# Second FFN matrix of a two-layer streaming encoder by seven block products, with an adding transfer for one weight sum

## Chip, cores and metric

The kernel runs on one core of one Trainium2 chip. The metric is the device time of one execution in microseconds (us), from the first to the last instruction of the core and the little around it; of several runs the median is given.

## What is computed

One step of an encoder of two layers on 544 tokens (512 of a prompt, 32 of a later chunk) with 1024 features. Cut to what matters here:

```python
def swiglu(x, w_in, w_out):                  # w_in 1024 x 5632, w_out 2816 x 1024
    gate, up = jnp.split(x @ w_in, 2, axis=-1)
    return (jax.nn.silu(gate) * up) @ w_out

def encoder_layer(x, ...):
    x = layer_norm(ALPHA * x + 0.5 * swiglu(x, w_ffn_in[0], w_ffn_out[0]), ln_g[0], ln_b[0])
    ...                                      # mix = mixers(x @ w_in) @ w_out
    x = layer_norm(ALPHA * x + mix, ln_g[1], ln_b[1])
    x = layer_norm(ALPHA * x + 0.5 * swiglu(x, w_ffn_in[1], w_ffn_out[1]), ln_g[2], ln_b[2])
```

So there are four FFNs, two in each layer, with a mixer between the two. All is float32.

## The kernel before

Features lie on the 128 partitions, tokens on the free dimension: x is 8 tiles of 128 features x 544 tokens, and a matmul covers one half of the tokens, 272 columns (`HS`). For float32 accuracy each operand is split into a rounded high part (ACT, `S.activation` with Copy, L174 for weights, L286 for data) and the rest (DVE, L175, L287), and each product is three matmuls: high x high, low x high, high x low (L254, L258, L342).

An FFN has 22 inner features of 128 (`NF`). `plan` (L573) sets the order: `FSPLIT = (8, 7, 7)` cuts the inner features into three parts; a part's features are made, then, one feature later, the part's share of the second matrix (w2) is added to y for all 8 outputs. Below, a *w1 unit* is one inner feature, a *w2 stage* one part's pass over the outputs.

- **First matrix.** Features 0 and 1 (`NPLAIN`) are plain products. Features 2 to 21 are made by seven products of blocks in place of eight (`seven` L333, `hidden` L547): the blocks are the two halves of the 8 inputs, the two token halves, and gate and up. `Blocks.add` (L313) makes the sums of x's blocks once for an FFN (four DVE operations of 272 columns and two splits per pair of tiles), `Weights.sums` (L209) the sums of the weights' blocks for each unit (four DVE operations of 512 columns, `add` L204, and seven splits). 84 matmuls make a unit.
- **Second matrix.** Plain: for each output m, n features x 2 halves x 3 matmuls, then two additions to y on DVE (`resid` L450).
- **Last part and layer norm** (`out_phase` L458). The third w2 stage carries the layer norm with it. After output 1 a rough mean of output 0 is taken by a matmul (`shift`, L371) and subtracted; from there on each finished output is shifted (DVE L378), squared (ACT L380), and added into two sums by POOL (`add`, L381 and L382). POOL also prepares the held back outputs (`before`, L389). The last two outputs (four in the kernel's last norm) are held back as `tail`: half 0 of all of them first, added on DVE (`add_last` L394 to L397), then the statistics of half 0 by matmuls (`stats` L403, L408), the centring and scaling (`centre` L427, `spread` L419 and L422, `scale` L433, L438), and the new x (ACT L443, POOL L444). `start` (L525) begins the next matrix's first two products, tile by tile, as the new x comes.
- **Weights.** `Weights` (L158) loads on the SP queue, in the order of use, into 3 raw tiles of 1024 columns (`RAW_BUFS`), and splits into 10 pairs of tiles of 512 columns (`W_BUFS`). `get` keeps one or two units ahead of the use (`ahead`, L235).

Each engine executes in order; the program's scheduler sets that order from the code and the tiles that come free.

Of the kernel before, what the change touches and what calls it, by code (L numbers as in the profile page):

```python
# [10 lines left out]
F32 = mybir.dt.float32  # L11
# [59 lines left out]
def encoder_kernel(  # L71
# [6 lines left out]
    w2: bass.AP,  # L78
    wi: bass.AP,
# [19 lines left out]
    xp = ctx.enter_context(tc.tile_pool(name="xp", bufs=34))  # L99
# [48 lines left out]
    class Tile:  # L148


        def __init__(self, groups):
            self.groups = groups

        def at(self, k):
            g, c = k // 4, k % 4
            return tuple(v[:, c * P:(c + 1) * P] for v in self.groups[g])

    class Weights:  # L158

# [6 lines left out]
        def fetch(self):  # L166
            return wp.tile([P, NK * P], F32, tag="raw", name="raw", bufs=RAW_BUFS)

        def group(self, raw):

            n = raw.shape[-1]
            hi = wp.tile([P, G], F32R, tag="whi", name="whi", bufs=W_BUFS)
            lo = wp.tile([P, G], F32R, tag="wlo", name="wlo", bufs=W_BUFS)
            S.activation(out=hi[:, :n], in_=raw, func=AF.Copy)  # L174
            V.tensor_tensor(out=lo[:, :n], in0=raw, in1=hi[:, :n].bitcast(F32), op=ALU.subtract)  # L175
            return hi, lo

        def blocks(self, src):
            out = []
            for i in range(2):  # L180
                raw = self.fetch()
                nc.sync.dma_start(out=raw, in_=src[:, 2 * i * G:2 * (i + 1) * G])
                out += [raw[:, :G], raw[:, G:]]
            return out

        def load(self):
            kind, src, n = self.units[self.loaded]
            self.loaded += 1
            if kind == "t":
                raw = self.fetch()  # L190
                nc.sync.dma_start(out=raw[:, :n], in_=src)
                out = Tile([self.group(raw[:, g:min(g + G, n)]) for g in range(0, n, G)])
            elif kind == "p":
                out = self.pair([self.group(b) for b in self.blocks(src)])
            else:
                out = self.sums(src)
            self.ready.append(out)

        @staticmethod
        def pair(groups):  # L200
            b11, b12, b22, b21 = groups
            return [Tile([b11, b21]), Tile([b12, b22])]

        def add(self, a, b):  # L204
            r = big["pool"].tile([P, G], F32, tag="sum", name="sum", bufs=4)
            V.tensor_tensor(out=r, in0=a, in1=b, op=ALU.add)  # L206
            return r

        def sums(self, src):  # L209
            b11, b12, b22, b21 = self.blocks(src)  # L210
            g11, g21 = self.group(b11), self.group(b21)
            r1 = self.add(b11, b12)
            r2 = self.add(r1, b22)
            g2, g1 = self.group(r2), self.group(r1)
            g3 = self.group(self.add(b12, b22))
            g22 = self.group(b22)
            return g11, g21, g2, g1, g3, g22, self.group(self.add(r2, b21))

        def first(self, x):

            src, n = self.units[0][1], G
            out = []
            for i in range(NK // 4):
                ks = slice(4 * i, 4 * i + 4)
                nc.sync.dma_start(out=ya[:, ks, HS[0]], in_=xT[:, ks, HS[0]])
                raw = self.fetch()
                for c in range(2):
                    nc.sync.dma_start(out=raw[:, c * n:(c + 1) * n], in_=src[:, (2 * i + c) * n:(2 * i + c + 1) * n])
                for k in range(NK)[ks]:
                    split(y[k], x[k], HS[0])  # L230
# [908 lines left out]
```

## Time and profile before

| | us |
|---|---|
| median of 3 runs | 2022.68 |
| lowest, highest | 2021.6, 2023.53 |
| the profiled execution | 2021.5 |
| its span, first to last instruction | 2019.7 |
| mean granted TensorE clock, share of full speed | 0.985 |
| stages of the first FFN, by PE: w1 features 2 to 8 | 44.13 to 118.51 |
| first w2 stage (8 features) | 118.51 to 166.51 |
| w1 features 9 to 15 | 166.51 to 240.06 |
| second w2 stage (7 features) | 239.90 to 281.98 |
| w1 features 16 to 21 | 281.98 to 345.02 |
| third w2 stage with the norm, up to the mixer's first matmul | 344.86 to 391.23 |

The profile is one execution. Its views: a page of totals; windows, which give each engine's busy time in a stretch; groups of instructions by line; a timeline; the waits; the chain of work that ended last, followed backwards. A duration on PE or DVE overlaps its neighbours, so the cost of one more instruction is read from the distance between starts.

### The profile page before, as it was taken

Reading aid. Unit: us, or ns where it says so; the run is one execution under the profiler, and the core shown is the slowest. Engines: PE = TensorE matmul, PEld = TensorE weight load, DVE = VectorE, ACT = ScalarE, POOL = GpSimd, SP = SyncE. Lnnn points to the kernel's source line nnn. Section 1 sums busy time; section 2 is a strip of 40 time slices with the busy share of each in tenths; the row PEclk is TensorE's granted clock in tenths of the full one; section 3 lists DMA queues with packets and bytes.
Section 4 is the critical chain, followed back from the end, with each engine's and each line's share of the span. In section 5 each row is a group of like instructions: output and inputs, shape, how many; then the busy total and the mean of one; then the engine's idle time right before and its main releaser. Section 6 shows DMA issues by size and latency. Waiting matters only on the chain.

```text
span 2019.7 us, 37955 instructions
## 1 busy us (share of the span) xinstructions
PE 1974.7 (98%) x15326; PEld 1935.6 (96%) x15326; DVE 1476.5 (73%) x2854; ACT 1002.9 (50%) x2009; POOL 225.1 (11%) x216
## 2 busy tenths in 40 slices
PE   7999999999998999999999999999999989999997
PEld 7999999999998999999999999999999989999997
DVE  7957767777658966858698586777766599577677
ACT  5634535465435543526366254455644366345353
POOL 0000000510224000000320000015001320000003
PEclk9999999999999999999999999999999999999999
DMA  6332323142221332323313323232421213323231
GB/s 199 105 105 85 105 85 110 58 152 92 64 84 32 115 105 84 100 87 101 100 52 107 94 95 109 81 104 85 136 96 55 84 39 108 105 84 105 88 102 45
DMA packets 61752, 189.09 MB, mean 94 GB/s; under 512 B 8932, under 2 KB 13156, under 8 KB 61576
## 3 DMA queue, kind: packets, MB, share of 16 engines
q1 hardware_dynamic: 52592, 173.18, 27.0%
q10 hardware_dynamic: 8984, 13.49, 2.1%
q8 instruction: 120, 1.97, 0.4%
q14 instruction: 56, 0.46, 0.1%
HBM read 179.88 MB, written 8.34 MB: 93 GB/s over the span
## 4 chain that ended last, share of the span: by engine, by line
PE 89%; DVE 6%; ACT 2%; DMA 1%; issue 1%; POOL 1%; SPq 0%; ACTq 0%
PE b L342 41%; PE b L254 28%; PE b L258 14%; DMA raw<-in_w 1%; PE b L773 1%; PE b L772 1%; DVE wlo L175 1%; PE o L788 1%; DVE z L433 1%; POOL xl L444 1%; ACT ya L438 1%; ACT whi L174 1%; DVE sum L206 1%; DVE ya L427 1%; PE b L753 0%
## 5 line engine op out<-in xcount | busy, mean ns | idle before, releaser
L174 ACT ACTIVATE whi<-raw 128x512 fp32r<-128x512 f32 x576 | 353.8, 618 | 510.8 <-PE b L258 304.6
L175 DVE TENSOR_TENSOR wlo<-raw,whi 128x512 fp32r<-128x512 f32 x576 | 403.2, 703 | 165.6 <-ACT whi L174 161.7
L254 PE MATMUL b<-hh,whi 128*128 128x272 f32 x1408 | 405.7, 288 | 0.0
L254 PE MATMUL b<-hh,wlo 128*128 128x272 f32 x1408 | 405.5, 288 | 0.0
L258 PE MATMUL b<-hl,whi 128*128 128x272 f32 x1408 | 404.7, 287 | 0.0
L174 ACT ACTIVATE whi<-sum 128x512 fp32r<-128x512 f32 x320 | 200.9, 631 | 210.8 <-PE b L258 100.0
L254 PE MATMUL b<-xh,whi 128*128 128x272 f32 x896 | 270.4, 306 | 24.8 <-ACT sg L591 12.2
L175 DVE TENSOR_TENSOR wlo<-sum,whi 128x512 fp32r<-128x512 f32 x320 | 218.7, 688 | 87.4 <-ACT whi L174 79.9
L342 PE MATMUL b<-xh,wlo 128*128 128x272 f32 x960 | 276.2, 288 | 0.0
L342 PE MATMUL b<-xh,whi 128*128 128x272 f32 x960 | 276.1, 288 | 0.0
L342 PE MATMUL b<-xl,whi 128*128 128x272 f32 x960 | 275.2, 287 | 0.0
L254 PEld LDWEIGHTS b<-hh,whi 128*128 128x128 f32 x1408 | 265.0, 188 | 0.1
L254 PEld LDWEIGHTS b<-hh,wlo 128*128 128x128 f32 x1408 | 264.9, 188 | 0.1
L258 PEld LDWEIGHTS b<-hl,whi 128*128 128x128 f32 x1408 | 264.8, 188 | 0.0
L254 PE MATMUL b<-xh,wlo 128*128 128x272 f32 x896 | 261.7, 296 | 0.3 <-DVE wlo L175 0.3
L258 PE MATMUL b<-xl,whi 128*128 128x272 f32 x896 | 248.1, 297 | 1.4 <-POOL xl L444 1.4
L254 PEld LDWEIGHTS b<-xh,whi 128*128 128x128 f32 x896 | 175.1, 196 | 30.5 <-ACT xh L443 13.5
L342 PE MATMUL b<-s56h,whi 128*128 128x272 f32 x640 | 184.5, 288 | 1.3 <-ACT up L552 1.3
L342 PE MATMUL b<-s73h,whi 128*128 128x272 f32 x640 | 184.6, 288 | 0.6 <-ACT sg L552 0.6
L342 PE MATMUL b<-s56h,wlo 128*128 128x272 f32 x640 | 184.5, 289 | 0.0
L342 PE MATMUL b<-s73h,wlo 128*128 128x272 f32 x640 | 183.9, 287 | 0.0
L342 PE MATMUL b<-s73l,whi 128*128 128x272 f32 x640 | 183.9, 287 | 0.0
(220 smaller groups left out, 4177.7 us busy)
## 6 DMA issues: line engine op xcount, KB each, us to landing
raw<-in_w SPq DMA_DIRECT2D x206, 512.0 KB, 3.7
raw<-in_w SPq DMA_DIRECT2D x64, 448.0 KB, 3.3
raw<-in_wi SPq DMA_DIRECT2D x40, 512.0 KB, 3.3
raw<-in_wo SPq DMA_DIRECT2D x16, 512.0 KB, 3.3
U<-scr ACTq DMA_DIRECT2D x8, 320.0 KB, 3.4
out_nkT<-k ACTq DMA_DIRECT2D x8, 272.0 KB, 2.4
out_nvT<-vT ACTq DMA_DIRECT2D x8, 272.0 KB, 2.1
out_yT<-ya SPq DMA_DIRECT2D x16, 136.0 KB, 1.8
```

What stands on the lines that cost most here:

```text
L174: S.activation(out=hi[:, :n], in_=raw, func=AF.Copy)
L175: V.tensor_tensor(out=lo[:, :n], in0=raw, in1=hi[:, :n].bitcast(F32), op=ALU.subtract)
L206: V.tensor_tensor(out=r, in0=a, in1=b, op=ALU.add)
L254: PE.matmul(acc[:, :HALF], v, x[k][0][:, HS[h]], start=first and i == 0, stop=False)
L258: PE.matmul(acc[:, :HALF], w.at(k)[0], x[k][1][:, HS[h]], start=False, stop=last)
L342: PE.matmul(acc[:, :HALF], v[:, cs], x, start=opens and j == 0 and m == 0, stop=j == len(xs) - 1 and m == 2, skip_group_check=True)
L427: eng.tensor_tensor(out=c, in0=c, in1=self.mean[h], op=ALU.subtract)
L433: V.tensor_tensor(out=z, in0=c, in1=self.rstd[h], op=ALU.mult)
L438: S.activation(out=c, in_=z, func=AF.Identity, bias=b, scale=g)
L444: POOL.tensor_tensor(out=xl[:, sl], in0=c, in1=xh[:, sl].bitcast(F32), op=ALU.subtract)
L772: PE.matmul(g[:, :w], qc[c][parts[c], qs], kh[parts[c], :w], start=True, stop=False)
L773: PE.matmul(g[:, :w], qc[c][:, qs], kc[c][:, :w], start=False, stop=True)
```

## The change

The second matrix is also computed by seven products for 18 of the 22 inner features. `FSPLIT = (6, 6, 6, 4)`: three parts of 6 features by seven products, the last 4 features plainly, in `out_phase`. The blocks are pairs of outputs (m, m+1), pairs of inner features (even, odd), and token halves. `Blocks.add` now also makes the sums of a pair of inner features (L327 to L330 of the changed kernel), and `resid7` adds the seven products to y. A unit of w2 has three column groups per block, so 384 columns. In `sums` one of the four additions, r3 = b12 + b22, is made by a DMA transfer that POOL issues and that adds onto the loaded tile; the others are laid out on double tiles of 1024 columns, the splits still on at most 512 columns each. Features 0 and 1 come as plain tiles, the sums of x's blocks are made after feature 0 is evacuated, and buffers are cut anew: 4 raw tiles, 4 double pairs, 26 instead of 34 tiles of data plus 16 of one half.

```diff
-FSPLIT = (8, 7, 7)
+FSPLIT = (6, 6, 6, 4)
-W_BUFS = 10
-RAW_BUFS = 3
+W_BUFS = 4
+RAW_BUFS = 4
...
-        def sums(self, src):
-            b11, b12, b22, b21 = self.blocks(src)
-            g11, g21 = self.group(b11), self.group(b21)
-            r1 = self.add(b11, b12)
-            r2 = self.add(r1, b22)
-            g2, g1 = self.group(r2), self.group(r1)
-            g3 = self.group(self.add(b12, b22))
-            g22 = self.group(b22)
-            return g11, g21, g2, g1, g3, g22, self.group(self.add(r2, b21))
+        def part(self, raw, hi, lo):
+            n = raw.shape[-1]
+            for c in (slice(0, n // 2), slice(n // 2, n)) if n > G else (slice(0, n),):
+                S.activation(out=hi[:, c], in_=raw[:, c], func=AF.Copy)
+                V.tensor_tensor(out=lo[:, c], in0=raw[:, c], in1=hi[:, c].bitcast(F32), op=ALU.subtract)
...
+        def sums(self, src, n):
+
+            a, b = self.fetch()[:, :2 * n], self.fetch()[:, :2 * n]
+            u, v = slice(0, n), slice(n, 2 * n)
+            nc.sync.dma_start(out=b, in_=src[:, 2 * n:])
+            nc.sync.dma_start(out=a, in_=src[:, :2 * n])
+            POOL.dma_start(out=b[:, u], in_=src[:, 3 * n:], accum_op=ALU.add)
+            ga = self.group(a)
+            r = big["pool"].tile([P, 2 * G], F32, tag="sum", name="sum", bufs=2)[:, :2 * n]
+            V.tensor_tensor(out=r[:, u], in0=a[:, u], in1=b[:, u], op=ALU.add)
+            V.tensor_tensor(out=r[:, v], in0=r[:, u], in1=b[:, v], op=ALU.subtract)
+            gr, gb = self.group(r), self.group(b)
+            V.tensor_tensor(out=a[:, v], in0=r[:, u], in1=a[:, v], op=ALU.add)
+            g4 = tuple(wp.tile([P, G], F32R, tag=f"{t}4", name=f"{t}4", bufs=1)[:, :n] for t in ("hi", "lo"))
+            self.part(a[:, v], *g4)
+            return [tuple(t[:, c] for t in g) for g in (ga, gr, gb) for c in (u, v)] + [g4]
...
+    def resid7(m, alpha):
+
+        seen = set()
+
+        def step(i, h, op):
+            def f(acc):
+                c = y[m + i][:, HS[h]]
+                if alpha and (i, h) not in seen:
+                    V.scalar_tensor_tensor(out=c, in0=c, scalar=ALPHA, in1=acc, op0=ALU.mult, op1=op)
+                else:
+                    V.tensor_tensor(out=c, in0=c, in1=acc, op=op)
+                seen.add((i, h))
+            return f
...
     def ffn(l, f, x, pre):
-        xb = Blocks(x)
-        hs = []
+        xb = Blocks(x[:NK // 2], x[NK // 2:])
...
-                hs.append(new_x("h"))
-                split(sg, hs[-1])
+                n = i - starts[last]
+                if n >= 0:
+                    tail.append(new_x("h") if n else new_b("h"))
+                    split(sg, tail[-1])
+                elif i % 2 == 0:
+                    if i in starts:
+                        parts.append(Blocks([], []))
+                    hb = parts[-1]
+                    hb.first.append(new_h("h", 1))
+                    split_half(sg, hb.first[-1], 0)
+                    held = sg
+                else:
+                    hb.second.append(new_x("h"))
+                    split(sg, hb.second[-1])
+                    hb.add(held, sg, new_x)
+                if i == 0:
+                    for k in range(NK // 2):
+                        xb.add(y[k], y[k + NK // 2], new_b)
                 continue
...
-            for m in range(NK):
-                acc = run(mm2(W.get(), part, range(n)))
-                for h in range(2):
-                    resid(m, acc[h], h, i == 0)
+            if i == last:
+                return out_phase(l, 2 * f, tail, range(FSPLIT[i]), False)
+            for m in range(0, NK, 2):
+                seven(W.get(), parts[i], resid7(m, i == 0))
```

What the instructions' order becomes is shown at two places. The first is DVE in the first w2 stage. Names: ya is y, wlo the low part of a weight, sum and raw the sums and loaded blocks of weights, b a PSUM bank. Before:

```order
L454 SCALAR_TENSOR_TENSOR ya<-ya,b 128x272
L175 TENSOR_TENSOR wlo<-raw,whi 128x512
L454 SCALAR_TENSOR_TENSOR ya<-ya,b 128x272
L206 TENSOR_TENSOR sum<-sum,raw 128x512
L175 TENSOR_TENSOR wlo<-raw,whi 128x512
L206 TENSOR_TENSOR sum<-raw 128x512
L454 SCALAR_TENSOR_TENSOR ya<-ya,b 128x272
L175 TENSOR_TENSOR wlo<-raw,whi 128x512
L206 TENSOR_TENSOR sum<-sum,raw 128x512
L454 SCALAR_TENSOR_TENSOR ya<-ya,b 128x272
```

Now, from the middle of one pair of outputs to the middle of the next:

```order
L208 TENSOR_TENSOR raw<-sum,raw 128x384
L600 SCALAR_TENSOR_TENSOR ya<-ya,b 128x272
L602 TENSOR_TENSOR ya<-ya,b 128x272
L177 TENSOR_TENSOR wlo<-sum,whi 128x384 x2
L600 SCALAR_TENSOR_TENSOR ya<-ya,b 128x272
L205 TENSOR_TENSOR sum<-raw 128x384
L600 SCALAR_TENSOR_TENSOR ya<-ya,b 128x272
L177 TENSOR_TENSOR wlo<-raw,whi 128x384 x2
L602 TENSOR_TENSOR ya<-ya,b 128x272
L206 TENSOR_TENSOR sum<-sum,raw 128x384
L602 TENSOR_TENSOR ya<-ya,b 128x272
L177 TENSOR_TENSOR wlo<-raw,whi 128x384 x2
```

Two additions to y and a split or sum alternated before, and the sums belonged to the next w1 unit; now ten operations on weights of 384 columns and seven additions stand in each pair of outputs, and the sum of raw blocks (L205), which needs the adding transfer, stands between additions of the pair before it.

The second place is POOL at the passage from the mixer to the second FFN. Before (L413 is a power for the norm, L444 the low part of the new x, L389 the next norm):

```order
L413 TENSOR_TENSOR rstd<-var,mhalf 68x4
L444 TENSOR_TENSOR xl<-ya,xh 128x272 x5
L413 TENSOR_TENSOR rstd<-var,mhalf 68x4
L444 TENSOR_TENSOR xl<-ya,xh 128x272 x11
L389 TENSOR_TENSOR ya<-ya,shift 128x544 x2
```

Now (L423, L454 the same; L202 is the adding transfer):

```order
L423 TENSOR_TENSOR rstd<-var,mhalf 68x4
L454 TENSOR_TENSOR xl<-ya,xh 128x272 x4
L423 TENSOR_TENSOR rstd<-var,mhalf 68x4
L454 TENSOR_TENSOR xl<-ya,xh 128x272 x11
L202 DMA raw<-in_w 128x512
L454 TENSOR_TENSOR xl<-ya,xh 128x272
L202 DMA raw<-in_w 128x512 x3
L202 DMA raw<-in_w 128x384 x4
```

An adding transfer has moved ahead of the last of sixteen low parts, and the others follow in the stages in which POOL had no instruction.

## Rows read from the trace of the kernel before

**Rows 1.** The page, part 1: each engine's busy time, share and instructions.
```profile
PE 1974.7 (98%) x15326; PEld 1935.6 (96%) x15326; DVE 1476.5 (73%) x2854; ACT 1002.9 (50%) x2009; POOL 225.1 (11%) x216
```

**Rows 2.** The page, part 4: the chain that ended last, by engine and by line.
```profile
PE 89%; DVE 6%; ACT 2%; DMA 1%; issue 1%; POOL 1%; SPq 0%; ACTq 0%
PE b L342 41%; PE b L254 28%; PE b L258 14%; DMA raw<-in_w 1%; PE b L773 1%; PE b L772 1%; DVE wlo L175 1%; PE o L788 1%; DVE z L433 1%; POOL xl L444 1%; ACT ya L438 1%; ACT whi L174 1%; DVE sum L206 1%; DVE ya L427 1%; PE b L753 0%
```

**Rows 3.** Windows by stage: from:to and length, each engine's busy us (instructions), clock, DMA.
```profile
118.51:166.51 48.00, 48.00 (x387) 48.00 (x386) 23.24 (x42) 10.78 (x17) 0.00 (x0) 1.00 0.27 87
166.51:240.06 73.55, 73.55 (x591) 73.55 (x590) 61.92 (x110) 44.34 (x83) 0.00 (x0) 1.00 0.32 98
...
344.86:391.23 46.37, 44.27 (x360) 43.83 (x358) 32.48 (x60) 18.79 (x35) 20.01 (x13) 1.00 0.27 87
```

**Rows 4.** Timeline of PE: start, us, line, operation, tiles, count [idle before].
```profile
355.34 0.41 PE L371 MATMUL o<-rough,ones 128*128 128x272 f32 x2
...
383.27 0.62 PE L403 MATMUL o<-acc,onesd 128*128 128x272 f32 x2
...
391.23 0.40 PE L254 MATMUL b<-xh,whi 128*128 128x272 f32 x1 [2.11 <-ACT xh L443]
```

**Rows 5.** Timeline of POOL in the same stage.
```profile
356.71 3.72 POOL L389 TENSOR_TENSOR ya<-ya,shift 128x544 f32<-128x544 f32 x2 [356.27 <-DVE wlo L175]
...
373.41 1.69 POOL L381 TENSOR_TENSOR acc<-acc,ya 128x544 f32<-128x544 f32 x1 [1.80 <-DVE ya L378]
...
379.92 1.38 POOL L382 TENSOR_TENSOR acc<-acc,sq 128x544 f32<-128x544 f32 x1
```

**Rows 6.** Groups by line of POOL: count | busy us, mean ns | idle.
```profile
L382 POOL TENSOR_TENSOR acc<-acc,sq 128x544 f32<-128x544 f32 x28 | 41.3, 1475 | 0.0
L381 POOL TENSOR_TENSOR acc<-acc,ya 128x544 f32<-128x544 f32 x22 | 35.5, 1615 | 37.5 <-DVE ya L378 37.5
```

**Rows 7.** Timelines of POOL, DVE, PE in the last FFN's end.
```profile
1971.98 5.03 POOL L389 TENSOR_TENSOR ya<-ya,shift 128x544 f32<-128x544 f32 x3 [327.31 <-DVE wlo L175]
...
1986.65 1.35 POOL L382 TENSOR_TENSOR acc<-acc,sq 128x544 f32<-128x544 f32 x1
...
1986.72 1.59 DVE L396 TENSOR_TENSOR acc<-acc,ya 128x272 f32<-128x272 f32 x1 [1.98 <-POOL acc L381]
...
1993.40 0.62 PE L403 MATMUL o<-acc,onesd 128*128 128x272 f32 x2
```

**Rows 8.** Window of DVE where the second FFN begins: busy us (instructions), PEclk, DMA.
```profile
640.00:693.60 53.60, 53.06 (x101) 1.00 0.25 79
```

**Rows 9.** Window of PE behind the hole at 391.23: busy us (instructions), PEclk, DMA.
```profile
391.23:398.10 6.87, 6.87 (x38) 0.54 0.00 0
```

**Rows 10.** Waits of PE: us in total, times, longest us.
```profile
PE b L254 <- ACT sg L591: 12.2, 3, 8.1
```

**Rows 11.** DMA issues: count, KB each, median us to landing.
```profile
raw<-in_w SPq DMA_DIRECT2D x206, 512.0 KB, 3.7
...
ck<-in_ckT ACTq DMA_DIRECT2D x8, 256.0 KB, 4.3
...
Us<-scr ACTq DMA_DIRECT2D x8, 68.0 KB, 2.9
par_sb<-in_par SPq DMA_DIRECT2D x1, 474.0 KB, 10.0
```

**Rows 12.** Timeline of DVE in a w2 stage.
```profile
257.31 0.43 DVE L456 TENSOR_TENSOR ya<-ya,b 128x272 f32<-128x272 f32 x1
257.65 0.55 DVE L175 TENSOR_TENSOR wlo<-raw,whi 128x384 fp32r<-128x384 f32 x1
258.12 0.69 DVE L206 TENSOR_TENSOR sum<-raw 128x512 f32<-128x512 f32 x1
258.72 0.69 DVE L206 TENSOR_TENSOR sum<-sum,raw 128x512 f32<-128x512 f32 x1
```

**Rows 13.** Groups by line of DVE.
```profile
L175 DVE TENSOR_TENSOR wlo<-raw,whi 128x384 fp32r<-128x384 f32 x64 | 38.9, 608 | 12.2 <-ACT whi L174 10.7
```

More of the change, by code (lines that the diff above doesn't have):

```diff
@@ L189, in load @@
             if kind == "t":
[L190 to L194, printed above, removed]
-            else:
[L196 to L202, printed above, removed]
@@ L229, in first @@
                 for k in range(NK)[ks]:
-                    split(y[k], x[k], HS[0])
-                out += [self.group(raw[:, c * n:(c + 1) * n]) for c in range(2)]
-            self.loaded, self.ready = 1, [self.pair(out)]
+                    split_half(y[k], x[k], 0)
+                for raw, (hi, lo) in zip(raws, groups):
+                    self.part(raw[:, cs], hi[:, cs], lo[:, cs])
+            self.loaded, self.ready = 2, [Tile(g) for g in groups]
             nc.sync.dma_start(out=ya[:, :, HS[1]], in_=xT[:, :, HS[1]])
@@ L240, in get @@
         def get(self, n=None):
+            self.used += 1
             if n is None:
[L242 to L243 removed]
+                kind, _, cols = self.units[min(self.used, len(self.units) - 1)]
+                n = 1 if kind == "s" else 2 if cols > G else 3
             self.ahead(n)
             return self.ready.pop(0)
[L247 to L249 removed]
     def mm_h(acc, w, x, k, h, first):
         for i, v in enumerate(w.at(k)):
[L254 removed]
+            PE.matmul(acc[:, :HALF], v, x[k].at(0, h), start=first and i == 0, stop=False)
     def mm_l(acc, w, x, k, h, last):
[L258 removed]
+        PE.matmul(acc[:, :HALF], w.at(k)[0], x[k].at(1, h), start=False, stop=last)
     def mm(acc, w, x, ks, h):
@@ L495, in out_phase @@
         if not ln.final:
-            ln.x = [new_x("x") for _ in range(NK)]
+            ln.x = new_xs()
         g = tail_mm(1, 1)
@@ L580, in plan @@
         yield 2, len(FSPLIT) - 1
+    def resid7(m, alpha):
[9 more added lines that the diff above has]
+            return f
+        add, sub = ALU.add, ALU.subtract
+        return [step(0, 0, add), step(0, 0, add), step(1, 0, sub), step(1, 1, add), step(1, 1, sub), step(1, 0, add),
+                step(0, 1, add)]
     def ffn(l, f, x, pre):
-        xb = Blocks(x)
-        hs = []
+        xb = Blocks(x[:NK // 2], x[NK // 2:])
+        last = len(FSPLIT) - 1
+        starts = [sum(FSPLIT[:s]) for s in range(last + 1)]
+        parts, tail = [], []
         for what, i in plan():
@@ L587, in ffn @@
                 if i < NPLAIN:
-                    ua, ga = pre if i == 0 else [run(mm2(w, x, range(NK))) for w in W.get()]
+                    ua, ga = pre if i == 0 else [run(mm2(W.get(), x, range(NK))) for _ in range(2)]
                     sg = tmp("sg")
@@ L1018, in encoder_kernel @@
     W = Weights(units)
-    x = [new_x("x") for _ in range(NK)]
+    x = new_xs()
     warm = side()
```

131 lines of the change are left out of this document (65 added, 66 removed).

## Prediction

> **What bounds the kernel now.** I read the busy shares first: PE is busy for 1974.7 us of the 2019.7 us span, DVE for 1476.5, POOL for 225.1 [rows 1]. The chain that ended last agrees: 89% of it is PE, and 41% is L342 (seven products), 28% L254 and 14% L258 (plain products) [rows 2]. The reader is to see that PE streams with almost no hole, so a matmul that goes away on PE gives its time back, as long as nothing else ends later there. The stages then give the price of a matmul: 48.00 us for the 384 plain matmuls of the first w2 part, 73.55 us for 588 of seven w1 units, so **125.1 ns** from start to start [rows 3] (the tables count a few neighbours as well). In those stages DVE is busy for 23.24 of 48.00 us and 61.92 of 73.55 us; it has room in the first kind and little in the second.
>
> Two places are not bound by PE. At the end of each FFN the layer norm runs through POOL, DVE and ACT, and in the stretch around an FFN's first feature DVE is full: 53.06 of 53.60 us from 640.00 on [rows 8].
>
> The sum is made against the profiled execution, 2021.5 us (span 2019.7 and 1.8 around it). The median of the runs, 2022.68, is 1.2 above it; the forecast is moved by that at the end. About 0.2% (4 us) is what a measurement of this kernel can tell from no change.
>
> **Matmuls removed: -54 us.** Plainly, 18 features cost 18 x 8 outputs x 2 halves x 3 = 864 matmuls in each FFN. By seven products, a part of 6 features costs 4 pairs of outputs x 7 x 3 x 3 = 252, three parts 756. That is 108 fewer, 432 over four FFNs; times 0.125 us = 54.0 us. The w1 units keep 84 matmuls.
>
> **The layer norm at the end of each FFN: +35 us.** Part of that gain is not on the path. Of an FFN's 108 matmuls, the earlier parts give none: 384 + 336 plain ones become 756, 4.5 us more. The last part gives 144: from 7 features to 4, 336 matmuls become 192, 18.0 us less. But this stage holds the norm's chain, which does not shrink. In the first one (344.86 to 391.23, 46.37 us [rows 3]) the rough mean's matmul comes after two outputs, 84 matmuls, at 355.34 [rows 4]; POOL starts at 356.71 and ends at 381.30 [rows 5]; the statistics' matmul follows at 383.27 and the next matrix at 391.23 [rows 4]. In the trace POOL waits for DVE ahead of the later pairs (1.80 us in the row shown), and the statistics come when PE arrives, 306 matmuls in. After the change the rough mean is due after 48 matmuls, 6.0 us into the stage, and PE is at the statistics after 180, at 22.9 with the norm's own matmuls. POOL starts 1.4 us after the rough mean and has 3.72 us of L389 and five pairs of L381 and L382 of 1.615 + 1.475 us [rows 5, 6], 19.2 us in one piece: it ends at 26.6. Then come the last additions on DVE (381.30 to 383.27, 2.0) and the same 7.96 us to the next matrix: 36.5 at most, 35.8 if POOL and DVE disturb one another less. So the stage saves about 10.3 of its 18.0 us and loses 7.7. I take 7.5 for each of the three FFNs that have such a stage, 22.5. In the last FFN, four outputs are held back: POOL ran from 1971.98 to 1988.00 and the statistics started at 1993.40, 33.3 us into the stage at 1960.06 [rows 7]. After it, POOL may start at 7.4, ends at 23.4, and DVE's additions for the four outputs (one set after POOL, the others as PE delivers, 1986.72 to 1993.40 now, some 5 us when PE is ahead) put the statistics at about 28.4. It saves 4.9 of 18.0, 13 lost. Together 35. The bounds: 20, if POOL's operations take their shortest values (1.37 and 1.36 us of [rows 5]: 5 x 0.36 = 1.8 us less, and as much again behind it), and 44, if each longer hole in PE brings a slow stretch. For that there is a row: after the 2.11 us hole at 391.23 [rows 4] the granted clock is 0.54 for 6.87 us, the lower level of 1.2 GHz, in which 38 matmuls ran [rows 9]; 38 x 0.125 = 4.8, so 2.1 us each and 8.4 for four.
>
> **The starts of the four FFNs: +7 us.** Feature 0 is now evacuated ahead of the block sums of x, so PE's three waits on L591 (12.2 us together, 8.1 the longest [rows 10]) shrink; but the block sums then fall behind, on a DVE that is full there [rows 8], with one more split and four more additions per pair of features. The order on POOL shows a new wait: in the second FFN of a layer an adding transfer stands ahead of the last xl (L454), and it waits until the block's own load has landed, 3.7 us behind its issue [rows 11]. I take 4 us twice, 2 for the fuller DVE in the third FFN, -3 at startup: +7, between -8 (the waits go, nothing follows) and +15.
>
> **DVE in the steady stages: nothing, but little is left.** DVE gains 664 instructions, mostly additions and splits of 272 to 544 columns, about 250 us: 1476 becomes some 1730 us. Prices are from start to start where DVE does not wait: 0.60 us for 512 columns (258.12 to 258.72), 0.47 for 384 (257.65 to 258.12), 0.34 for 272 (257.31 to 257.65) [rows 12]. One pair of outputs of w2 needs ten operations on weights (7 splits, 3 sums) and 7 additions to y: 10 x 0.47 + 7 x 0.35 = 7.2 us, under 63 x 0.125 = 7.9 of PE. A w1 unit grows to some 9.6 us on average (more in odd features, where the block sums are made) under 10.5. Covered by PE, with 8 to 9% to spare; if that cover went, 48 units of w2 would each cost what they lack. The DVE rows' own durations are the other bound: a mean of 0.608 for 384 [rows 13] and 0.43 for 272 [rows 12] give 9.1 us and +58 us for 48 units. I take the start-to-start prices, since [rows 12] stand in just such a w2 stage.
>
> The Trainium skill (VectorE: DVE Perf Modes, "The TRN2 errata") gives (N+151)/0.96 ns for an addition of N columns in fp32, and so speaks against splitting the weights into more, shorter operations: by it 384 columns are 557 ns, 272 are 441, and a pair of outputs 8.7 us, an estimate that would make DVE the bound. The trace agrees with it as a duration (0.55 and 0.69 us in [rows 12]), not as a price, since the next operation starts 0.08 us before it ends.
>
> **The adding transfer: +5 us.** r3 = b12 + b22 leaves DVE; POOL now issues a transfer that adds a block of 192 KB onto the one that has landed (256 KB in w1). No row shows such a transfer. The nearest loads land 2.9 us (68 KB), 3.7 (512 KB) and 4.3 us (256 KB) after issue, the slowest 10.0 (474 KB, at startup) [rows 11]. It decides through a loop: a raw tile comes free after b's splits, the load takes 3.4 (between those of 68 and 512 KB by its 384), the adding transfer T, then the sum on DVE, an addition and the two splits, 1.9: T + 5.3 us per pair of outputs against 7.9 on PE. So T over 2.6 binds; but the last of a unit's seven tiles is due only at its seventh product, 6 us behind its first, and that lead has to be used up in some 3.5 turns of a stage. Up to 2.6 + 6/3.5 = 4.3 us it is free; above, 12 stages x 3.5 turns = 42 us for each us of T. At 2.9 the cost is 0, at 4.3 about 0, at 10.0 some +240. I take 4.3, nearest in kind and size, with 5 us for the ones that land later.
>
> By the Trainium skill (DMA: Bandwidth & Descriptors, "Anatomy of one DMA — SWDGE (gpsimd) path") a transfer from this engine takes 2.0 us and its bytes over 436 GB/s, here an estimate of 2.5 us, and the term would be 0; nothing in this trace shows it.
>
> **Sum:** -54 + 35 + 7 + 5 = -7, so 2014.5 us for the profiled execution and, 1.2 above it, a median of **2015.7**.
>
> **Rivals.**
>
> - *The whole gain arrives* (0.12): POOL is not late, for instance as its pairs run closer than now, and the starts gain. For it: POOL is 11% busy and idles between pairs. Against it: 19 us of work behind the rough mean, in a stage of 24 us. -54 + 10 = -44: 1979.
> - *The adding transfer is late* (0.20), slower: from T = 4.6 us on it eats the forecast's gain; at 5.5 it costs 1.2 x 42 = 50 and the time is 2022.7 - 12 + 50 = 2061; DVE, which executes in order, then stands at the sum (L205) with splits of the unit in progress behind it, and PE at those. For it: the destination must be read too, POOL makes the request by program, and loads of 256 KB take 4.3 us already [rows 11]. Against it: the transfers of 512 KB land in 3.7, and the 16 DMA engines are busy for 27 to 32% in these stages [rows 3].
> - *DVE becomes the bound* (0.10): durations, not starts, count when sums, splits and evacuations alternate and each waits for another engine. By [rows 12] a pair of outputs is then 10 x 0.55 + 7 x 0.43 = 8.5 us, 48 x (8.5 - 7.9) = 29, and 2015.7 + 29 = 2045. For it: 0.608 in [rows 13]. Against it: the starts in [rows 12]. The Trainium skill's page VectorE: DVE Perf Modes, cited above, is the rule of this case.
> - *Nothing to be told* (0.13): the slow stretches of the clock and later block sums take the rest: 2015.7 + 8, 2023.
> - *Forecast as summed* (0.45): 2004 to 2020.
>
> **Numbers.** Faster by over 0.2% (under 2018.6): nearly all of the forecast (0.42) and the first rival (0.12), so 0.54; within 0.2% 0.16; slower 0.30 (late transfer, DVE, a share of the fourth). The range leaves out most of the whole-gain case and the far part of a late transfer: **1990 to 2045**; the likeliest case's own range is 2004 to 2020.
>
> **What would show it.** Right: PE's matmuls 432 fewer, w2 units 7.9 us apart, PE waiting about 5 us at the statistics (L413 of the changed kernel) in each FFN's end, with POOL's pairs without idle before it; DVE busy near 1730 us. Wrong: waits of DVE's L205 on a raw tile's transfer of tens of us in all, PE L352 waiting on wlo in w2 stages, adding transfers that land later than 4.3 us, or w2 units further apart than 8.

## The result and the profile after

The changed kernel takes 2152.53 us (median of 4 runs, 2151.45 to 2154.78) against 2022.97 us before in the same session: ratio 1.064, 95% interval 1.0625 to 1.0656. That is 130 us slower, where 2015.7 was forecast in a range from 1990 to 2045. The profiled execution has a span of 2153.0 us, and all accounts below are made from spans.

The busy shares of the changed kernel (the page's first part) answer to [rows 1]:

```profile
PE 1986.9 (92%) x14894; PEld 1919.6 (89%) x14894; DVE 1713.1 (80%) x3518; ACT 1082.0 (50%) x2259; POOL 356.7 (17%) x344
```

DVE grew to 1713 us, near the 1730 that were expected, and POOL from 225 to 357 us. The matmuls are fewer by the 432 that were counted, yet the span is longer: PE has holes. Windows of the first FFN (columns as in [rows 3]: length, busy us of PE, PEld, DVE, ACT and POOL, granted clock, DMA share, GB/s) show a w2 stage of four units, the w1 stage behind it, and the last part with the norm:

```profile
95.74:134.24 38.50, 34.22 (x262) 32.92 (x261) 31.17 (x69) 14.66 (x30) 3.45 (x4) 1.00 0.46 118
134.24:201.05 66.81, 63.56 (x499) 62.53 (x499) 57.96 (x115) 38.80 (x78) 5.17 (x6) 1.00 0.44 111
...
379.65:419.24 39.59, 29.92 (x217) 28.51 (x215) 32.88 (x52) 15.40 (x31) 22.66 (x13) 0.87 0.26 87
```

The w2 stage takes 38.50 us for 252 matmuls, at 0.125 us each 31.5. DVE is busy for only 31.17 of the 38.50. The reader is to see that neither PE nor DVE is full there: both wait.

What they wait for, the waits show. Of PE (us in total, times, longest):

```profile
PE b L352 <- DVE ya L602: 44.1, 28, 2.7
PE b L352 <- DVE sg L577: 35.5, 20, 2.8
PE o L413 <- DVE acc L406: 34.5, 6, 7.6
...
PE b L352 <- ACT sg L621: 4.8, 1, 4.8
...
PE b L352 <- DVE ya L600: 3.3, 3, 1.3
...
PE b L352 <- DVE wlo L177: 0.6, 2, 0.4
```

L602 and L600 are operations that empty PSUM banks into y (in w2), L577 one that empties them into sg (in w1), and L406 is the norm's. For the low parts of weights (wlo), which the prediction had named, PE waits 0.6 us in all. DVE in turn has one large wait:

```profile
DVE sum L205 <- DMA raw<-in_w: 132.4, 71, 3.7
```

By shape (count | busy us, mean ns | idle before), 89.7 us of it lie in w1 and 42.8 in w2:

```profile
L205 DVE TENSOR_TENSOR sum<-raw 128x512 f32<-128x512 f32 x80 | 55.2, 690 | 91.6 <-DMA raw<-in_w 89.7 <-issue 1.9
...
L205 DVE TENSOR_TENSOR sum<-raw 128x384 f32<-128x384 f32 x48 | 26.7, 556 | 42.8 <-DMA raw<-in_w 42.8
```

L205 is the first sum of a unit's weights and needs the adding transfer. In the trace, each of PE's 51 waits on L602, L577 and L600 (82.9 us) comes together with a wait of DVE at L205, or at most 2.5 us behind one: that is the chain from the transfer to PE, in w1 as in w2. The transfers' landing times (DMA issues of the changed kernel: count, KB, median us from issue to landing) answer to [rows 11]:

```profile
raw<-in_w SPq DMA_DIRECT2D x174, 512.0 KB, 3.8
...
raw<-in_w POOLq DMA_DIRECT2D x80, 256.0 KB, 5.4
...
raw<-in_w POOLq DMA_DIRECT2D x48, 192.0 KB, 4.5
raw<-in_w2t SPq DMA_DIRECT2D x32, 256.0 KB, 2.6
```

**T is 4.5 us in w2 and 5.4 in w1**, where I had taken 4.3 from a plain load of 256 KB; in this run a plain load of 256 KB on SP's queue lands in 2.6. The timeline of DVE in the first w2 stage then shows the loop (start, us, idle before and its releaser):

```profile
101.78 0.56 DVE L205 TENSOR_TENSOR sum<-raw 128x384 f32<-128x384 f32 x1 [1.47 <-DMA raw<-in_w]
...
111.47 0.56 DVE L205 TENSOR_TENSOR sum<-raw 128x384 f32<-128x384 f32 x1 [1.76 <-DMA raw<-in_w]
...
119.73 0.44 DVE L600 SCALAR_TENSOR_TENSOR ya<-ya,b 128x272 f32<-128x272 f32 x1 [0.32 <-PE b L352]
122.29 0.69 DVE L205 TENSOR_TENSOR sum<-raw 128x512 f32<-128x512 f32 x1 [2.13 <-DMA raw<-in_w]
122.90 1.02 DVE L177 TENSOR_TENSOR wlo<-raw,whi 128x384 fp32r<-128x384 f32 x2
123.84 0.78 DVE L602 TENSOR_TENSOR ya<-ya,b 128x272 f32<-128x272 f32 x2
```

From one first sum to the next 9.69 us pass (101.78 to 111.47), where PE needs 7.9; over all 36 such turns within w2 stages the mean is 9.85. At 120.16 DVE stands for 2.13 us; an addition of a product to y (L602) stands behind it and runs only at 123.84. The timeline of PE in the same place:

```profile
122.14 0.28 PE L352 MATMUL b<-hl,whi 128*128 128x272 f32 x1
124.42 0.36 PE L352 MATMUL b<-hh,hi 128*128 128x272 f32 x1 [2.00 <-DVE ya L602]
```

PE waits 2.00 us for exactly that addition, because the PSUM bank is not free.

The account by stage, from the starts of the first matmul of each stage (an FFN from its first feature up to its last part; the last part with the norm, up to the next matrix's first matmul or the end; and the rest, which is the two mixers and the startup), is, for all four FFNs:

| span, us | up to the last part | last part and norm | rest | all |
|---|---|---|---|---|
| before | 1337.5 | 200.9 | 481.3 | 2019.7 |
| after | 1490.4 | 175.8 | 486.8 | 2153.0 |
| difference | +152.9 | -25.1 | +5.5 | +133.3 |
| forecast | +30 | -37 | 0 | -7 |

(The forecast's +30 is 18 for the matmuls that move into the earlier parts, 7 for the starts, 5 for the transfer; its -37 is 72 less 35.) So 123 of the 140 us by which the sum was off lie in the feature and w2 stages, 12 in the norm, 5 in the mixers.

### The profile page after: what moved, and what is told of

The parts are those of the page before. It is cut to its first block, busy times and chain, and to the rows that moved or that the text cites. A ratio compares the mean times of both kernels' runs of the same rounds, so it can differ in the third digit from the quotient of the medians.

```text
span 2153.0 us, 38435 instructions
## 1 busy us (share of the span) xinstructions
PE 1986.9 (92%) x14894; PEld 1919.6 (89%) x14894; DVE 1713.1 (80%) x3518; ACT 1082.0 (50%) x2259; POOL 356.7 (17%) x344
## 5 line engine op out<-in xcount | busy, mean ns | idle before, releaser
L176 ACT ACTIVATE whi<-raw 128x512 fp32r<-128x512 f32 (+1 forms) x688 | 383.2, 594 | 468.2 <-PE b L352 262.6
L177 DVE TENSOR_TENSOR wlo<-raw,whi 128x512 fp32r<-128x512 f32 (+1 forms) x688 | 465.6, 705 | 54.9 <-ACT whi L176 50.9
L202 POOL DMA_DIRECT2D raw<-in_w x128 | 111.0, 867 | 1211.6 <-DVE lo L177 329.7
L352 PE MATMUL b<-s73h,whi 128*128 128x272 f32 x928 | 278.2, 300 | 13.9 <-DVE ya L602 10.4
L352 PE MATMUL b<-s56l,whi 128*128 128x272 f32 x928 | 267.4, 289 | 0.0
L176 ACT ACTIVATE whi<-sum 128x512 fp32r<-128x512 f32 (+1 forms) x256 | 139.6, 583 | 127.9 <-PE b L352 108.8
L352 PEld LDWEIGHTS b<-s73h,whi 128*128 128x128 f32 x928 | 174.4, 188 | 26.1 <-issue 7.9
L205 DVE TENSOR_TENSOR sum<-raw 128x512 f32<-128x512 f32 (+1 forms) x128 | 81.9, 640 | 134.4 <-DMA raw<-in_w 132.4
L352 PEld LDWEIGHTS b<-s56h,whi 128*128 128x128 f32 x928 | 175.2, 190 | 7.5 <-ACT sg L621 5.0
L245 PEld LDWEIGHTS b<-xh,wlo 128*128 128x128 f32 x896 | 175.9, 196 | 1.1 <-DVE wlo L177 0.4
L249 PEld LDWEIGHTS b<-xl,whi 128*128 128x128 f32 x896 | 167.8, 195 | 10.1 <-POOL xl L454 9.4
```

What stands on the lines that cost most here:

```text
L176: S.activation(out=hi[:, c], in_=raw[:, c], func=AF.Copy)
L177: V.tensor_tensor(out=lo[:, c], in0=raw[:, c], in1=hi[:, c].bitcast(F32), op=ALU.subtract)
L202: POOL.dma_start(out=b[:, u], in_=src[:, 3 * n:], accum_op=ALU.add)
L205: V.tensor_tensor(out=r[:, u], in0=a[:, u], in1=b[:, u], op=ALU.add)
L245: PE.matmul(acc[:, :HALF], v, x[k].at(0, h), start=first and i == 0, stop=False)
L249: PE.matmul(acc[:, :HALF], w.at(k)[0], x[k].at(1, h), start=False, stop=last)
```

## The experiments

Theory A: the adding transfer stands in a loop with DVE, which works in order, and PE gets its PSUM banks late. Rival B: DVE is simply full. Rival C: the added traffic and POOL's requests slow the other transfers. The last rows of this section give all runs' accounts together.

**r3 on DVE.** The added block is in SBUF already, as the other half of the same raw tile.

```diff
-            POOL.dma_start(out=b[:, u], in_=src[:, 3 * n:], accum_op=ALU.add)
+            V.tensor_tensor(out=b[:, u], in0=b[:, u], in1=b[:, v], op=ALU.add)
```

> Edit: r3 = b12 + b22 is made by a DVE addition of the two loaded halves in place of POOL's adding transfer (80 of 512 and 48 of 384 columns, some 72 us more on DVE). Theory A (the adding transfer lies in the loop of the raw tile, DVE stands at the sum L205 until it lands, and the evacuations of PSUM behind it come late): the waits of L205 on a transfer fall from 132 us to under 20, w2 units go from 9.6 us to 7.9 to 8.3, and the time to 2020 to 2045. Theory B (DVE is the bound, 1713 us busy and in order): with 72 us more on DVE the time stays at 2150 or grows. Theory C (the software queue's traffic slows the other loads): as A here, the fourth run tells it apart.

Measured: 2043.14 us, ratio to before 1.0104 (1.0089 to 1.0119), inside theory A's range. DVE has 128 operations more and the kernel is 109 us faster than the changed one: rival B falls. Groups of DVE by line in this run (count | busy us, mean ns | idle before):

```profile
L202 DVE TENSOR_TENSOR raw<-raw 128x512 f32<-128x512 f32 x80 | 55.7, 696 | 6.8 <-DMA raw<-in_w 6.8
...
L205 DVE TENSOR_TENSOR sum<-raw 128x512 f32<-128x512 f32 x80 | 54.8, 685 | 0.9 <-DMA raw<-in_w 0.9
```

The first operation that needs the loaded blocks (L202) waits 6.8 us for transfers in all its 80 operations of w1, L205 0.9. The first sums of w2 units are 8.32 us apart on average, where they were 9.85; these turns hold some matmuls of w1 as well. Windows of PE and the others in the first w2 stage with the w1 stage's beginning, and behind it:

```profile
94.80:137.16 42.36, 42.36 (x338) 42.20 (x337) 41.29 (x92) 19.11 (x40) 0.00 (x0) 1.00 0.34 101
137.16:192.56 55.40, 55.17 (x434) 54.37 (x433) 54.38 (x108) 34.37 (x69) 0.00 (x0) 1.00 0.30 95
```

PE is busy for 42.36 of 42.36 us, so the stage is PE's again; DVE is busy for 41.29 of them. PE's waits on L602 fall to 0.3 us, and L577 is no longer among them.

**r3 on POOL.** The same line, with POOL for V.

> Edit: the same addition on POOL, from the two loaded halves. Theory A: an addition of 512 columns on POOL is about 1.5 us (1.475 to 1.615 for 544 in the trace of before) against 5.4 for the transfer, so the loop falls well under PE's time: 2010 to 2035, a little better than on DVE. Theory B: 2150 less nothing. If POOL's additions and DVE's disturb each other (L389 on POOL and L378 on DVE did), DVE operations with two operands in SBUF get longer and it is slower than the DVE version: over 2045.

Measured: 2105.31 us (1.0409, 1.0393 to 1.0424), a miss. Groups by line in this run:

```profile
L202 POOL TENSOR_TENSOR raw<-raw 128x512 f32<-128x512 f32 x80 | 133.7, 1672 | 647.4 <-DMA raw<-in_w 378.4 <-DVE lo L177 78.2 <-DVE wlo L177 51.2
...
L177 DVE TENSOR_TENSOR lo<-raw,hi 128x512 fp32r<-128x512 f32 x80 | 72.2, 903 | 2.4 <-ACT hi L176 1.0
```

POOL's addition of 512 columns took 1.67 us on average, so the latency is gone, but DVE's additions and splits beside it lengthen: L208 from 687 to 857 ns, the split of the seventh block from 689 to 903, DVE's busy time to 1795 us (1769 with 128 more operations on DVE). The price of contention, which I had as the exception, was the case. That these lengths make the whole of the 62 us against r3 on DVE is argued, not shown.

**r3 on DVE in w2 alone, and in w1 alone.** The same line under a condition on n (384 columns in w2, 512 in w1).

> Edit: the DVE addition only in the 48 units of w2; the 80 units of w1 keep the adding transfer. The stages of after lose 77 us in w2 and 65 in w1 against 125.4 ns a matmul. Theory A: what w2 lost comes back and w1's stays: 2075 to 2095. If the loss in w1 is only w2's backlog, carried over, both come back: under 2045.

> Edit: the complement of the run with the DVE addition in w2 only: here the 80 units of w1 make r3 on DVE and the 48 of w2 keep the adding transfer. If the two losses add up (after 2152.5, w2 alone mended 2088.5, both mended 2043.1): 2152.5 - 45.4 = 2107, with w1 units at PE's pace and w2 units still 9.6 us apart. If the w1 loss is w2's backlog carried over, w1 units stay slow behind each w2 stage and the time is over 2125.

Measured: 2088.51 us (1.0322, 1.0300 to 1.0343) and 2069.94 us (1.0240, 1.0225 to 1.0256). The first fits; the second is 37 us better than additive. Mending w2 gives 64 us, mending w1 gives 83, both give 109. So the losses overlap. A likely reason, which no run isolates, is that a w1 unit that comes late leaves the next w2 stage less in hand, and the other way round. The larger one is w1's, for which the prediction had no term at all.

**The sums before the transfer.**

```diff
-            POOL.dma_start(out=b[:, u], in_=src[:, 3 * n:], accum_op=ALU.add)
...
-            V.tensor_tensor(out=r[:, u], in0=a[:, u], in1=b[:, u], op=ALU.add)
-            V.tensor_tensor(out=r[:, v], in0=r[:, u], in1=b[:, v], op=ALU.subtract)
+            V.tensor_tensor(out=r[:, v], in0=a[:, u], in1=b[:, u], op=ALU.add)
+            V.tensor_tensor(out=r[:, u], in0=r[:, v], in1=b[:, v], op=ALU.add)
+            POOL.dma_start(out=b[:, u], in_=src[:, 3 * n:], accum_op=ALU.add)
```

> Edit: the adding transfer stays, with all its bytes, but two of the three sums on DVE are made before it from the loaded blocks (r1 = b11 + b12, r2 = r1 + b22), so only the splits of r3 need it. Theory A (the harm is that DVE stands at the first sum until the transfer lands, and PSUM's evacuations behind it): the waits of L205 on a transfer go from 132 to under 40 us, w2 and w1 units to nearly PE's 7.9 and 10.5 us, the time to 2020 to 2045. Theory A2 (it harms anywhere in the raw tile's loop, since the tile comes free as late as before): the wait moves to the splits and the time stays over 2110. Theory C (the transfer's traffic and POOL's requests slow others): over 2110 too, without such waits.

Measured: 2101.11 us (1.0379, 1.0363 to 1.0394), between the two theories. Groups of DVE by line in this run:

```profile
L204 DVE TENSOR_TENSOR sum<-raw 128x512 f32<-128x512 f32 x80 | 54.9, 688 | 38.9 <-DMA raw<-in_w 38.7
...
L204 DVE TENSOR_TENSOR sum<-raw 128x384 f32<-128x384 f32 x48 | 26.6, 554 | 4.0 <-DMA raw<-in_w 3.0
```

In w2 the wait is nearly gone (4.0 us over 48 units), in w1 38.9 of 91.6 us stay. The total fell by 51 us, not by 109. PE's waits in this run show where the rest lies:

```profile
PE b L352 <- DVE sg L577: 20.5, 20, 2.7
...
PE b L352 <- DVE ya L602: 2.9, 5, 1.2
```

In w2 the late evacuations are gone (2.9 us, 44.1 in the changed kernel). In w1 20.5 of 35.5 us stay: by the trace 9.5 of them come with a wait of DVE at the first sum, now for the load of the raw tile itself, and 10.3 with a wait of DVE at a split (L177). So the order on DVE is part of the harm, and a transfer that only the splits need still delays the raw tile; how much each of the two costs was not separated.

**The transfers kept, nobody waiting.** r3 on DVE, and beside it POOL's adding transfers onto a spare tile that nobody reads; one tile of the pool xb is given up for it (with all 18 tiles, xb wanted 46.25 KB of a partition where 45.16 were left).

```diff
+            POOL.dma_start(out=self.junk[:, :n], in_=src[:, 3 * n:], accum_op=ALU.add)
+            V.tensor_tensor(out=b[:, u], in0=b[:, u], in1=b[:, v], op=ALU.add)
```

> Edit: r3 on DVE as in the first run, and the same adding transfers are still made by POOL, onto a tile that nobody reads (17 instead of 18 tiles of the pool xb, to make room). Theory A: nobody waits for them: 2043 within 12 us. Theory C: they slow the loads or DVE, 2080 or more.

Measured: 2280.00 us, by its number a case of theory C (2080 or more). But the loss has one place. The waits of DVE in this run:

```profile
DVE ya L408 <- POOL ya L403: 226.2, 1, 226.2
```

No longer tied to the units, the 128 transfers ran one behind the other in POOL's queue, each held only until the one before it had landed on the same tile, as POOL's timeline in the first w2 stage shows:

```profile
100.17 0.88 POOL L205 DMA_DIRECT2D junk<-in_w  x1 [4.35 <-DMA junk<-in_w]
104.57 0.87 POOL L205 DMA_DIRECT2D junk<-in_w  x1 [3.52 <-DMA junk<-in_w]
109.96 0.87 POOL L205 DMA_DIRECT2D junk<-in_w  x1 [4.51 <-DMA junk<-in_w]
```

At the end of the first FFN the norm's POOL work was queued behind them, 226 us. Up to that point a transfer was issued about every 5 us, in the changed kernel about every 10 (97.10, 107.21, 117.56 in the same stage), and the first FFN's stages took 318.6 us, the same as with r3 on DVE and none of them (318.6). The loads of 512 KB landed in 3.7 us there, as with r3 on DVE (3.7). So rival C falls for these stages: the traffic costs nothing that can be measured, the dependence does.

**Two half transfers.**

```diff
-            POOL.dma_start(out=b[:, u], in_=src[:, 3 * n:], accum_op=ALU.add)
+            for q in range(2):
+                c = slice(q * n // 2, (q + 1) * n // 2)
+                POOL.dma_start(out=b[:, c], in_=src[:, 3 * n + c.start:3 * n + c.stop], accum_op=ALU.add)
```

> Edit: the adding transfer is made as two of half the columns, so POOL issues twice (0.86 us each) and the second lands later; the bytes are the same. Theory A with my loop (load 3.4 + T + 1.9 us, one turn for each unit of w2, no lead): T grows by about 0.8 us and each of the 48 units of w2 by as much, 38 us, and the 80 units of w1 by up to as much, 0 to 64 us: 2180 to 2255, with the waits of L205 at 190 us or more. If the forecast's lead of 6 us in each stage existed, or DVE's own work set the pace, the time stays within 15 us of 2152.

Measured: 2164.02 us (1.0707, 1.0692 to 1.0721), 11 us more than the changed kernel. It did not double what it was meant to double. DMA issues of this run:

```profile
raw<-in_w POOLq DMA_DIRECT2D x160, 128.0 KB, 4.6
...
raw<-in_w POOLq DMA_DIRECT2D x96, 96.0 KB, 4.0
```

A half lands sooner, 4.6 and 4.0 us. The second half starts 0.54 us behind the first, and both have landed 5.37 us (w1) and 4.74 us (w2) after the first one's start, medians of the trace, where the whole transfer had 5.37 and 4.53: T grew by nothing in w1 and by 0.2 us in w2. The waits at the first sum (L207 here) are 135.4 us, not 190. By the letter this is the expectation's other case, within 15 us of the changed kernel. But 0.2 us more cost 48 x 0.2 = 10 us without a lead and 42 x 0.2 = 8 by the formula with one, so the run is too small a step to tell the two apart.

**The norm's sums on DVE.** On top of r3 on DVE, the lines L391, L392 and L399 with V for POOL.

> Edit: as the first run, and the layer norm's sums and the shift of the held back outputs (L391, L392, L399) run on DVE instead of POOL. In the first run PE stands 7.5 us before the statistics in each FFN's end, while POOL works for 22 us in one piece, an operation of 544 columns at 1.8 us, and DVE's splits beside it take 1.8 us instead of 0.69. Theory T1 (POOL's chain, drawn out by the contention with DVE, sets the end): 12 operations of 0.64 us on DVE replace it, the wait falls under 2 us, the stage from 39.6 to about 34 us and the time by 15 to 30 us, to 2013 to 2028. Theory T2 (DVE sets the end): it has 8 us more to do there, the stage stays or grows, 2040 to 2060.

Measured: 2028.49 us (ratio 1.0024, 1.0014 to 1.0034), 15 us faster than with r3 on DVE alone; 0.5 us above T1's range, and well under T2's. The changed kernel's POOL in its first norm, which answers to [rows 5]:

```profile
387.42 3.75 POOL L399 TENSOR_TENSOR ya<-ya,shift 128x544 f32<-128x544 f32 x2 [37.43 <-ACT shift L382]
391.12 1.87 POOL L391 TENSOR_TENSOR acc<-ya 128x544 f32<-128x544 f32 x1
392.94 1.82 POOL L392 TENSOR_TENSOR acc<-acc,sq 128x544 f32<-128x544 f32 x1
...
407.14 1.77 POOL L392 TENSOR_TENSOR acc<-acc,sq 128x544 f32<-128x544 f32 x1
```

and PE behind it, which answers to [rows 4]:

```profile
410.42 1.25 PE L413 MATMUL o<-acc,onesd 128*128 128x272 f32 x2 [7.53 <-DVE acc L406]
...
419.24 0.39 PE L245 MATMUL b<-xh,whi 128*128 128x272 f32 x1 [2.11 <-ACT xh L453]
```

POOL's L399, L391 and L392 stand in one piece from 387.42 to 408.91, 21.5 us, since each addition takes 1.8 us and not 1.48 or 1.62; PE waits 7.53 us. From 391.12 to 408.91 DVE is busy for 17.58 of 17.79 us, and its splits lengthen too (timeline of DVE in the changed kernel):

```profile
391.67 1.86 DVE L177 TENSOR_TENSOR wlo<-raw,whi 128x512 fp32r<-128x512 f32 x1
```

The run with the transfers unread has the same sums in one piece, in the norm that came late, while DVE did nothing but one addition at their end (busy 1.24 of 13.15 us). There they start 1.28 to 1.29 us apart:

```profile
603.25 1.65 POOL L395 TENSOR_TENSOR acc<-ya 128x544 f32<-128x544 f32 x1
604.53 1.64 POOL L396 TENSOR_TENSOR acc<-acc,sq 128x544 f32<-128x544 f32 x1
605.82 1.63 POOL L395 TENSOR_TENSOR acc<-acc,ya 128x544 f32<-128x544 f32 x1
```

So it is not their standing in one piece that makes them 1.8 us, but what runs beside them: DVE above all, whose splits lengthen with them and take 0.69 us again in that stage when the sums are on DVE. The timeline of PE in the run of this experiment, with the sums on DVE:

```profile
380.78 0.73 PE L413 MATMUL o<-acc,onesd 128*128 128x272 f32 x2 [2.85 <-DVE acc L406]
...
388.62 0.59 PE L245 MATMUL b<-xh,whi 128*128 128x272 f32 x1 [2.00 <-ACT xh L453]
```

The wait before the statistics (L413) is 2.85 us, where under 2 was expected, the stage 35.4 instead of 39.6 us, and the last norm 51.2 instead of 57.5.

**A longer last part.** On top of r3 on DVE, `FSPLIT = (6, 6, 4, 6)`, with the third part's blocks laid out for four features.

> Edit: as the first run, with parts (6, 6, 4, 6): 16 instead of 18 features by seven products, so 12 matmuls more in each FFN's sum (48 x 0.125 = 6 us more on PE), but a last part of 288 instead of 192 matmuls, as long as the norm's chain. If the forecast's reason is right (the norm's chain hides behind a long last part and 35 to 49 us are lost without it): the wait before the statistics falls from 7.5 us to under 2; the time is 2043 + 6 - 30 = 2015 to 2028. If the norm's chain is not what costs: 2043 + 6, some 2049.

Measured: 2016.36 us (0.9962, 0.9950 to 0.9974). The timeline of PE at the first norm:

```profile
380.09 0.70 PE L414 MATMUL o<-acc,onesd 128*128 128x272 f32 x2 [1.33 <-DVE acc L407]
...
387.37 0.60 PE L246 MATMUL b<-xh,whi 128*128 128x272 f32 x1 [2.10 <-ACT xh L454]
```

1.33 us of wait before the statistics (L414) instead of 7.5: the chain is hidden again by plain matmuls.

**The held back outputs' shift on DVE as well.** L399 with V for POOL, on top of that.

> Edit: as the run with parts (6, 6, 4, 6), and the shift of the held back outputs (L399, 3.7 us on POOL ahead of its sums) on DVE, where it takes 0.64 us each. PE still waits 1.3 to 2.6 us before the statistics there. If POOL's chain is what is left: those waits go, some 2 us at each of six norms and 3 more in the last: 2003 to 2012. If DVE is full there: 2016 or slower.

> Edit: the kernel of the run before once more, unchanged, for its profile. If the time holds: 2004 to 2011, with waits before the statistics (L414) of under 1 us each at the FFNs' ends, where the run with L399 on POOL had 1.3 to 2.6. If L399 on POOL was not what PE waited for, those waits are as long as there.

Measured: 2007.24 us (0.9929, 0.9915 to 0.9942), and again 2008.14 us (0.9933, 0.9919 to 0.9946): **0.7% faster than the kernel before**, the fastest of all. Of PE's waits in the second of the two:

```profile
PE o L414 <- DVE acc L407: 8.1, 6, 3.2
```

The waits before the statistics are 8.1 us in six places, against 11.8 with L399 on POOL; at the first three FFNs' ends 0.7, 1.3 and 0.6, where under 1 was expected.

**The second matrix plain, the rest kept.** On top of r3 on DVE: `FSPLIT = (8, 7, 7)` and w2 by plain products, as in the kernel before.

> Edit: the first run (r3 on DVE) with the second matrix undone: parts (8, 7, 7), w2 plain as before, while the changed buffers, sums and the order at the starts stay. It tells what seven products in w2 are worth by themselves. If the forecast's terms hold (-54 for the matmuls, +35 to 49 for the norm): the first run is 5 to 20 us faster than this one, 2048 to 2063 here. If the rest of the change costs nothing, this is the kernel before, 2023, and seven products in w2 lose 20 us by themselves even without the transfer.

Measured: 2037.05 us (1.0076, 1.0062 to 1.0090), between the two statements. So the new buffers and sums, without seven products in w2, cost 15 us; seven products in w2 as cut by the change then add 6 more, transfer aside. The waits of DVE in this run hold something else:

```profile
DVE sum L204 <- DMA raw<-in_w: 79.6, 61, 3.4
DVE raw L201 <- DMA raw<-in_w: 58.4, 27, 3.5
```

DVE stands 138 us for raw blocks, more than the 132.4 of the changed kernel, and PE's waits on L576 (L577 of the changed kernel) are 2.2 us. So it is not the length of DVE's wait that costs, but what PE needs from behind it.

All runs' spans by the same account:

| span, us | up to the last part | last part and norm | rest | all |
|---|---|---|---|---|
| r3 on DVE | 1380.5 | 177.6 | 487.4 | 2045.5 |
| r3 on POOL | 1439.9 | 177.0 | 486.7 | 2103.6 |
| r3 on DVE in w2 alone | 1425.9 | 175.6 | 484.8 | 2086.3 |
| r3 on DVE in w1 alone | 1403.8 | 177.1 | 487.7 | 2068.6 |
| sums before the transfer | 1435.9 | 175.7 | 487.0 | 2098.6 |
| transfers unread | 1380.9 | 408.8 | 487.7 | 2277.4 |
| two half transfers | 1501.4 | 176.4 | 486.9 | 2164.7 |
| r3 and norm's sums on DVE | 1386.1 | 157.7 | 479.7 | 2023.5 |
| r3 on DVE, (6, 6, 4, 6) | 1338.9 | 190.0 | 487.2 | 2016.1 |
| the same, L399 on DVE | 1337.2 | 183.4 | 484.9 | 2005.5 |
| r3 on DVE, w2 plain | 1344.5 | 202.9 | 485.1 | 2032.5 |

## Why the prediction was wrong

**The adding transfer, +5: the step that failed.** The loop that the prediction wrote down, T + 5.3 us for each unit of w2, was right: with the T of 4.5 that the profile shows it gives 9.8, and the mean of the 36 turns is 9.85. What was wrong stood behind it: "that lead has to be used up in some 3.5 turns of a stage. Up to 2.6 + 6/3.5 = 4.3 us it is free". No such lead protected PE: at T = 4.5 that formula charges 0.2 x 42 = 8 us. What DVE's stall delays is not only weights that are due later, but the emptying of PSUM banks that stands behind the sum in DVE's order and that PE needs within the unit; the timeline at 119.73 to 124.42 shows it, and PE waited 82.9 us for such evacuations and 0.6 for low parts of weights. Without the lead the formula gives 48 x (9.8 - 7.9) = 91 us for w2 alone, were each unit to pay; mending w2 alone brought back 64. And the prediction applied the loop to w2 only: the 80 units of w1, with T = 5.4 us, had no term, and mending them alone brought back 83 us. Taking the transfer out of the loop, in both, moved the stages by 109.9 us (1490.4 to 1380.5); the 27 us of them beyond the 82.9 of these waits are laid to no line. The rival of the late transfer had the right sign, and DVE standing at L205 with PE behind it; but it saw splits in between, not evacuations, and its price was the formula with the lead: 2061 at T = 5.5, where T was 5.4 in w1 and 2152.5 was measured. Whether more than four raw tiles would have opened the loop, with the transfer kept, was not tried.

**The transfer's price by the Trainium skill.** The Trainium skill (DMA: Bandwidth & Descriptors, "Anatomy of one DMA — SWDGE (gpsimd) path") gave an estimate of 2.5 us by its fit of 2.0 us and the bytes over 436 GB/s. The trace disagrees: 4.5 us for 192 KB and 5.4 for 256 KB, from issue to landing, adding ones, beside the other loads. The measurement decides. By the Trainium skill's fit the term was 0, further off than the forecast's +5.

**Matmuls, -54: right in count.** All 432 are gone; in the (6, 6, 4, 6) run 384 are. That each gives its 0.125 us back once nothing else ends later can't be read from the changed kernel, whose PE has holes.

**The norm, +35: right in mechanism, too small.** The gain in the last parts was 25.1 us instead of 72, so 47 were lost, above the prediction's upper bound of 44. The term that was mis-sized is POOL's: five pairs at 1.615 + 1.475 us, the means of a trace in which POOL and DVE often ran apart (in the first norm of the kernel before, from 360.44 to 381.30, DVE is busy for 15.25 and POOL for 15.27 of 20.86 us). Beside a DVE that is busy all the time they cost 1.8 us each, the statistics came 30.8 us into the stage (379.65 to 410.42) instead of 28.6, and the stage took 39.6 instead of 36.5 us. The runs on the norm show that POOL's chain sets the end there: both the sums on DVE and the longer last part give the time back. The slow stretch of the clock, which the prediction kept for its upper bound, came as well: at the statistics (L413), behind PE's 7.53 us of idling, the granted clock is 0.50, the lower level of 1.2 GHz, and the two matmuls take 1.25 us against 0.62 in [rows 4].

**DVE in the steady stages, nothing: right as to the bound.** 1713 us of work were expected as 1730, and DVE did not become the bound: with 72 us more it ran faster. But its cover was thin, as said: with r3 on DVE and no transfer the stages still took 36 us longer than with w2 plain (1380.5 against 1344.5), of which 18 are matmuls; the other 18 are laid to no cause.

**The starts, +7.** They can't be told apart from the transfers in the changed kernel. With r3 on DVE and w2 plain, the stages up to the last part are 7.0 us over before (1344.5 against 1337.5), which is the size, though not measured by itself. The rest, +5.5 us in the mixers, had no term. With the norm's sums on DVE it is 479.7, below before, so POOL's part in the mixers' norms weighs there; whether that made the +5.5 was not tried.

By the rule of the Trainium skill (VectorE: DVE Perf Modes, "The TRN2 errata") a w2 unit with r3 on DVE, 11 operations of 557 ns and 7 of 441, would be 9.2 us of DVE, an estimate over PE's 7.9. The trace disagrees: in that run's first w2 stage PE was busy for 42.36 of 42.36 us, and the first sums of w2 units stood 8.32 us apart on average. Starts, not durations, were the price.

## What to carry to other kernels

A wait that is added on an engine that works in order is not priced by when its own result is due, but by the most urgent instruction behind it; look in the order for PSUM evacuations there. A transfer in a loop is worth an engine's addition only if the loop's time with it, load, issue, landing and all, stays under the bound engine's, in every kind of unit that uses it. And matmuls removed from a stage that hides a chain come back only up to that chain's length, whose operations get longer when they stand beside another engine's: here a last part of 288 matmuls, with fewer matmuls saved, beat one of 192 by 27 us (2016.4 against 2043.1).

## What the runs showed of the hardware

- An adding transfer that POOL issued kept POOL busy for 0.87 us on average, and landed 5.4 us after issue for 256 KB, 4.6 for 128 KB, where a plain load on SP's queue landed in 2.6 for 256 KB and in 3.8 for 512 KB.
- POOL's additions of 544 columns started 1.8 us apart when they followed one another beside DVE's work, and 1.28 to 1.29 us apart when DVE stood still; a DVE split of 512 columns from SBUF beside them went from 0.69 to 1.86 us.
- Adding transfers twice as often as in the changed kernel, onto a tile that nobody reads, cost the first FFN's stages nothing that can be measured (318.6 us with and without).
